# A hybrid decoder layer: an untaken branch moved from behind the expert loop to between its 26th and 27th block, and two of the closing row sums moved to TensorE

## The chip, the cores and the metric

The kernel runs on one NeuronCore of a Trainium2 chip. The metric is device time in microseconds (us) of one execution; the median of three runs stands for the kernel. About 0.5% (4 us) is what a measurement of this kernel can tell from no change.

## What is computed

One layer of a decoder trunk on 512 prompt rows and 8 sample rows of 1024 columns: a mixed attention and convolution stage, then a mixture of 32 experts of which each row uses 2, then a final RMSNorm. The change touches the end of the expert stage and the final norm only:

```python
hid = jax.nn.silu(jnp.einsum('nd,edf->nef', hf, w_gate)) * jnp.einsum('nd,edf->nef', hf, w_up)
y = jnp.einsum('nef,ne,efd->nd', hid, combine.astype(hid.dtype), w_down)
...
x = x + mods[5] * hier_moe(h, ...)
...
y_prompt = rmsnorm(xp, final_g)
y_sample = rmsnorm(xs, final_g)
```

## The kernel before, in words

The routed rows are sorted by expert into blocks of 64 rows. `run` (L1688) works off a list `todo` of 36 blocks: 6 experts whose weights were loaded ahead (blocks 0 to 5), then 4 experts with two blocks each (6 to 13), then 22 experts with one block each (14 to 35). An expert's weights are three tiles of 1 MB (`eg`, `eu`, `ed`), loaded by the SP queue (`weights`, L1609) into a rotating pool of 21 pages; a load waits until TensorE has used the page's former tile.

Two blocks share one gathered tile of 128 rows (`xg`, tiles `mA` and `mB` in the trace, two buffers). `gather` (L1626) is an indirect DMA that Pool issues. On TensorE, which works strictly in the order that `chain` and `in_turn` write down, a block is: `turned` (L1631, the gathered tile transposed in two halves, once for two blocks), `up` (L1643, 16 pairs of matmuls into `pgu`), `flip` (L1658) of the block before and `down` (L1667) of the block before. ScalarE applies Silu (`hidden`, L1655), VectorE multiplies; VectorE scales the result into `ot` (L1676) and Pool scatters it to `yrow` in DRAM with an indirect DMA (L1677).

Experts with more rows than their blocks hold would have left-over blocks. They sit in a branch (`tc.If(nxv > 0)`, L1731) behind the loop; in this data their number `nxi` is 0 and the branch isn't taken, but every engine loads the number, compares and jumps. Instructions of different engines are ordered by semaphores; where a branch isn't taken, each engine raises its semaphores by what the skipped code would have added. For Pool's DMA semaphores that is an instruction of its own, which the trace calls INC_SWDGE_SEM.

Then comes the closing stage (L1737 to L1795). SP loads the rows of `yrow` (two expert shares for each row, `yt`) when the scatters have landed; `xt` and the norm's gain `gf` were loaded before. For each of four tiles of 128 rows, `total` (L1752) adds `xt` and the two shares on VectorE and squares on ScalarE, Pool takes the inverse root (`pow`, L1765), and `final` (L1768) multiplies on VectorE and SP stores. `sample` (L1780) does the three additions and products for the 8 sample rows on Pool, between the tiles. `ORD` (L31) sets the order.

Of the kernel before, what the change touches and what calls it, by code (L numbers as in the profile page):

```python
# [9 lines left out]
F32 = mybir.dt.float32  # L10
# [3 lines left out]
AF = mybir.ActivationFunctionType  # L14
ALU = mybir.AluOpType
# [5 lines left out]
EPS = 1e-6  # L21
# [7 lines left out]
KTE = "VSSSSVVSSSSSSSVSSSSVVSSS"  # L29
GF_ = ()  # L30
ORD, ISS = "t0 t1 f0 t2 f1 s t3 q f2 f3", "fsq"  # L31
GT, TH, TF = (), (1, 1, 1, 2), (1, 1, 1, 2)
PLAN = ",c0,spread gn im sel,,,c1,k0 n cp,,,mc,,sn n3 n1 n0 n2,k1 rw,,,nq,,,,,,,,,,,,,cs,"
LU = (13, 15, 17)
EARLY = "CPXCACAXACAXCXAAICACAQCBIKI"
# [145 lines left out]
def body(tc, I, O, dbg=lambda *a: None):  # L181
# [1502 lines left out]
    def in_turn():  # L1684
        return tc.issue_after(chain[0].ins) if chain[0] is not None else ExitStack()


    def run(blocks, asks):  # L1688
        before = None
        for n, (b, W) in enumerate(blocks):  # L1690
            W = W()
            if n == 0:
                turned(b // 2, 0)
                turned(b // 2, 1)
            up(b, W, range(0, UP))
# [12 lines left out]
        down(*before)  # L1708

    pgus, hds, hTs_, scat = {}, {}, {}, []  # L1710
    chain = [lastw]
    asked = {0, OV0 // 2, NBLK // 2}
    gather(0)
# [2 lines left out]
    for j in range(NE):  # L1716
        hold = {}
        for _ in range(2 if NF <= j < NF + HV else 1):
            todo.append((len(todo), lambda j=j, hold=hold: hold.setdefault(0, hold.get(0) or weights(j))))
    run(todo, asked)  # L1720
    gfq = cp.tile([128, 256], F32, name="gfq", tag="c1")
    with tc.issue_after(mark["S"].ins):
        S.dma_start(gfq, I["GFQ"])
    gfb = page("gf")[:, 0:1024]
    SP.dma_start(gfb, I["GF"])
    xt = [page("xt0"), page("xt1")]
    for i in range(4):
        SP.dma_start(half(xt[i // 2], i % 2), xrow[128 * i:128 * i + 128])
    spare = [[page(f"sg{j}"), page(f"su{j}"), page(f"sd{j}")] for j in range(3)]
    nxv = nc.values_load(nxi[0:1, 0:1])  # L1730
    with tc.If(nxv > 0):  # L1731
        chain[0] = None
        gather(OV0 // 2)
        run([(b, lambda b=b: left(b - OV0)) for b in range(OV0, NBLK)], asked)


    ry = yrow.rearrange("(t a) f -> t (a f)", a=4)  # L1737
    ssf = cp.tile([128, 8], F32, name="ssf")
    rsf = cp.tile([128, 8], F32, name="rsf")
# [12 lines left out]
    def total(i):  # L1752
        t, t1, x = half(yt[i], 0), half(yt[i], 1), half(xt[i // 2], i % 2)
        (G if i in GT else V).tensor_tensor(x, x, t, op=ALU.add)
        n = 1024 // TH[i]
        for h in range(TH[i]):
            c = slice(n * h, n * h + n)
            op = V.tensor_tensor(t[:, c], x[:, c], t1[:, c], op=ALU.add)  # L1758
            S.activation(t1[:, c], t[:, c], AF.Square, scale=1.0 / 32, accum_out=ssf[:, 2 * i + h:2 * i + h + 1])  # L1759
        r = rsf[:, i:i + 1]  # L1760
        if TH[i] == 2:
            V.scalar_tensor_tensor(r, ssf[:, 2 * i:2 * i + 1], EPS, ssf[:, 2 * i + 1:2 * i + 2], op0=ALU.add, op1=ALU.add)
        else:
            V.tensor_scalar(r, ssf[:, 2 * i:2 * i + 1], EPS, None, op0=ALU.add)
        G.tensor_tensor(r, r, mh[:, 0:1], op=ALU.pow)  # L1765
        return op

    def final(i):  # L1768
        n = 1024 // TF[i]
        for h in range(TF[i]):  # L1770
            c = slice(n * h, n * h + n)
            t = half(yt[i], 0)[:, c]
            if i in GF_:
                S.activation(t, t, AF.Copy, scale=rsf[:, i:i + 1])
                G.tensor_tensor(t, t, gfb[:, c], op=ALU.mult)
            else:
                V.scalar_tensor_tensor(t, t, rsf[:, i:i + 1], gfb[:, c], op0=ALU.mult, op1=ALU.mult)  # L1777
            SP.dma_start(O[0][0, 128 * i:128 * i + 128, c], t)
# [6 lines left out]
    op = None
    for nm in ORD.split():
        with tc.issue_after(op.ins) if op is not None and nm[0] in ISS else ExitStack():
            r = (sample() if nm == "s" else quarter_rstd(rsf[:, 4:5], fs, 1.0 / D, EPS) if nm == "q" else
                 total(int(nm[1])) if nm[0] == "t" else final(int(nm[1])))
        if nm[0] == "t":  # L1790
            op = r
    V.scalar_tensor_tensor(fs, fs, rsf[:, 4:5], gfq, op0=ALU.mult, op1=ALU.mult)
# [26 lines left out]
```

## Time and profile before

| what | value |
|---|---|
| three runs | 795.72 us (median), 792.86, 796.38 |
| the profiled execution | 789.56 us, of it 787.8 us span |
| granted TensorE clock, mean | 0.944 of full speed |
| busy share of the span | TensorE 87%, VectorE 56%, ScalarE 27%, Pool 26% |
| HBM traffic | 267 GB/s over the span |

Times in the trace count from the span's start. "Releaser" is the work whose end let a waiting instruction go; a row's bracket gives the idle time of its engine before it. An instruction of a queue (SPq, POOLq, PEldq) is work of the engine's sequencer, not of the engine. Blocks of the expert loop are best counted by the ScalarE instruction `hd<-pgu` (L1655), which begins when a block's `up` is done: there are 36, from 522.1 to 746.7 us.

### The profile page before, as it was taken

Reading aid. Unit: us, or ns where it says so; the run is one execution under the profiler, and the core shown is the slowest. Engines: PE = TensorE matmul, PEld = TensorE weight load, DVE = VectorE, ACT = ScalarE, POOL = GpSimd, SP = SyncE. Lnnn points to the kernel's source line nnn. Section 1 sums busy time; section 2 is a strip of 40 time slices with the busy share of each in tenths; the row PEclk is TensorE's granted clock in tenths of the full one; section 3 lists DMA queues with packets and bytes.
Section 4 is the critical chain, followed back from the end, with each engine's and each line's share of the span. In section 5 each row is a group of like instructions: output and inputs, shape, how many; then the busy total and the mean of one; then the engine's idle time right before and its main releaser. Section 6 shows DMA issues by size and latency. Waiting matters only on the chain. (4 is left out here: it accounts for less than half of the span.)

```text
span 787.8 us, 12614 instructions
## 1 busy us (share of the span) xinstructions
PE 683.7 (87%) x4888; PEld 414.4 (53%) x4888; DVE 440.4 (56%) x960; ACT 213.7 (27%) x491; POOL 208.3 (26%) x182
## 2 busy tenths in 40 slices
PE   4999888997999988999789998289999999999910
PEld 3655777775786446644435444155555555554400
DVE  2444729999985758723776745843333333333245
ACT  1255721121113457634245323010110101010001
POOL 5134305035030101135602303312222222221114
PEclk9999999998999999999979999589999999999965
DMA  9985425644799303700004666679999999999954
GB/s 340 420 324 203 160 81 215 244 161 192 266 343 407 136 2 131 285 0 1 1 16 165 248 251 240 257 248 418 420 406 350 410 418 418 417 419 420 370 177 176
DMA packets 42332, 200.02 MB, mean 254 GB/s; under 512 B 10733, under 2 KB 14205, under 8 KB 22677
## 3 DMA queue, kind: packets, MB, share of 16 engines
q1 hardware_dynamic: 29341, 156.27, 50.7%
q0 software_dynamic: 10336, 40.95, 13.5%
q10 hardware_dynamic: 2592, 1.95, 0.8%
q8 instruction: 40, 0.66, 0.3%
q14 instruction: 23, 0.19, 0.1%
HBM read 187.82 MB, written 22.15 MB: 267 GB/s over the span
## 5 line engine op out<-in xcount | busy, mean ns | idle before, releaser
L591 DVE SCALAR_TENSOR_TENSOR y<-u,c,y 128x511 f32<-128x511 f32 (+23 forms) x120 | 103.7, 896 | 2.1
L1655 ACT ACTIVATE hd<-pgu 64x256 f32<-64x256 f32 x36 | 13.5, 375 | 200.4 <-PE pgu L1650 200.4
L1677 POOL DMA_INDIRECT yrow<-ot,six x36 | 39.1, 1085 | 99.4 <-DVE ot L1676 87.9
L1650 PE MATMUL pgu<-eu,mB 128*64 128x256 f32 x256 | 61.7, 384 | 1.9 <-DMA eu<-in_WU 1.9
L1650 PE MATMUL pgu<-eg,mB 128*64 128x256 f32 x256 | 62.2, 384 | 0.0
L1672 PE MATMUL pd<-ed,hTe 128*64 128x512 f32 x240 | 57.3, 598 | 0.8 <-issue 0.8
L1650 PE MATMUL pgu<-eu,mA 128*64 128x256 f32 x224 | 54.0, 384 | 1.8 <-DMA eu<-in_WU 1.8
L1650 PE MATMUL pgu<-eg,mA 128*64 128x256 f32 x224 | 54.2, 384 | 0.0
L1676 DVE SCALAR_TENSOR_TENSOR ot<-pd,wtb,mt 128x512 f32<-128x512 f32 x36 | 27.0, 751 | 44.3 <-PE pd L1672 44.3
L1656 DVE TENSOR_TENSOR hd<-pgu,hd 64x256 f32<-64x256 f32 x36 | 15.4, 428 | 59.1 <-ACT hd L1655 59.1
L1650 PEld LDWEIGHTS pgu<-eg,mB 128*64 128x64 f32 x256 | 32.8, 136 | 19.9 <-issue 5.1
L1381 ACT ACTIVATE P<-pSp,ast 128x128 f32<-128x128 f32 (+3 forms) x64 | 33.2, 534 | 24.2 <-DVE ast L1376 23.9
L1376 DVE TENSOR_REDUCE ast<-pSp 128x1 f32<-128x384 f32 (+3 forms) x44 | 27.3, 632 | 21.7 <-PE pSp L1371 21.6
L1650 PEld LDWEIGHTS pgu<-eg,mA 128*64 128x64 f32 x224 | 28.9, 136 | 17.3 <-issue 4.6
L225 DVE COPY hTe<-hTp 128x128 f32<-128x128 f32 x36 | 10.5, 291 | 48.3 <-PE hTp L1663 48.3
L370 PE MATMUL pr<-cTs,wc 128*64 128x256 f32 x256 | 37.1, 400 | 0.0
L1253 PE MATMUL woA<-wo,qT 128*128 128x512 f32 x64 | 35.9, 681 | 0.2 <-DVE rt L1175 0.2
L1650 PEld LDWEIGHTS pgu<-eu,mB 128*64 128x64 f32 x256 | 33.0, 136 | 4.0 <-DMA eu<-in_WU 2.8
L361 PE MATMUL cT<-CI,cR 128*128 128x128 f32 x128 | 21.1, 302 | 10.9 <-DVE cR L386 10.7
L1650 PEld LDWEIGHTS pgu<-eu,mA 128*64 128x64 f32 x224 | 28.9, 136 | 2.9 <-DMA eu<-in_WU 2.3
L1109 PE MATMUL woC<-wo,y 128*128 128x512 f32 x64 | 30.2, 605 | 0.1
L1413 PE MATMUL oT<-P,kv 128*64 128x512 f32 x80 | 28.6, 614 | 0.0
(572 smaller groups left out, 1654.5 us busy)
## 6 DMA issues: line engine op xcount, KB each, us to landing
eg<-in_WG SPq DMA_DIRECT2D x26, 1024.0 KB
eu<-in_WU SPq DMA_DIRECT2D x26, 1024.0 KB
ed<-in_WD SPq DMA_DIRECT2D x26, 1024.0 KB
wada<-in_WA SPq DMA_DIRECT2D x16, 1024.0 KB
wada<-in_WA POOLq DMA_DIRECT2D x8, 1024.0 KB, 15.2
WG<-in_WG SPq DMA_DIRECT2D x6, 1024.0 KB
WU<-in_WU SPq DMA_DIRECT2D x6, 1024.0 KB
WD<-in_WD SPq DMA_DIRECT2D x6, 1024.0 KB
```

What stands on the lines that cost most here:

```text
L361: PE.transpose(p[:, j, :], R[b:b + n, c, k, 2 * s8:2 * s8 + 2, :], ident[b:b + n, b:b + n])
L370: mark["PE"] = PE.matmul(self.pr[r][64 * c:64 * c + 64], wc1[:, c, 8 * r + 4 * h + s, :], self.T[h][:, c, s], start=(h == 0 and s == 0), s ...
L591: V.scalar_tensor_tensor(yb[:, s_:CVS], ub[:, :CVS - s_], w(k), yb[:, s_:CVS], op0=ALU.mult, op1=ALU.add)
L1109: PE.matmul(p, zc[:, g, 128 * i:128 * i + 128], wo[2 * n + 1][:, g], start=(g == 0), stop=(g == 3))
L1253: PE.matmul(pA, oTp[:, g, 128 * i:128 * i + 128], wo[2 * n][:, g], start=(g == 0), stop=(g == 3))
L1376: V.tensor_reduce(st[k][:, 0, h0:h0 + nh], pS[k][:, :nh * L].rearrange("p (h l) -> p h l", h=nh), axis=AX.X, op=ALU.max, negate=True)
L1381: S.activation(P[k][:, g, :L], pS[k][:, o:o + L], AF.Exp, bias=st[k][:, 0, g:g + 1], accum_out=st[k][:, 1, g:g + 1])
L1413: PE.matmul(oT[64 * k:64 * k + 64, :].rearrange("p (g t) -> p g t", g=4), kv12[:, br - 1, kt, 128 + 64 * k:192 + 64 * k], P[k][:, :, 128 * ...
L1650: chain[0] = PE.matmul(pgus[b][64 * h:64 * h + 64, :], xT[:, c, 64 * s_:64 * s_ + 64], w[:, c, :], start=(c == 0), stop=(c == 7))
L1672: chain[0] = PE.matmul(pd[64 * h:64 * h + 64, :], hT_[:, c, :], wd[:, c, 512 * h:512 * h + 512], start=(c == 0), stop=(c == 1))
L1676: V.scalar_tensor_tensor(ot, pd, wtb[:, b:b + 1], mt, op0=ALU.mult, op1=ALU.mult)
L1677: st = G.indirect_dma_start(out=yrow[:, :], out_offset=bass.IndirectOffsetOnAxis(ap=six[:, b:b + 1], axis=0), in_=ot, in_offset=None, boun ...
```

## The change

The list of blocks is cut after its first 26. `run` works off blocks 0 to 25, then the branch stands, then a second `run` works off blocks 26 to 35. The branch needs weight pages of its own; there were nine behind the loop, there are four now (`sg`, `su`, `sd0`, `sd1`), and they come out of the same rotating pool. Each `run` ends with its last block's `flip` and `down` and begins with its first pair's `turned`. In the closing stage, `yt` is loaded whole (four DMAs of 1 MB in place of eight of 512 KB), the sample rows are loaded by ScalarE's queue, and their work is on VectorE. The sums of tiles 0 and 2 (`TP`) are made by TensorE, as three matmuls with the unit matrix into one PSUM tile, for each half of the columns; VectorE adds tiles 1 and 3. The inverse roots of tiles 2 and 3 are taken by ScalarE's Sqrt and four small VectorE instructions; those of tiles 0 and 1 and of the sample rows stay on Pool. Orders on VectorE and ScalarE are written out (`dv`, `ac`).

```diff
-GT, TH, TF = (), (1, 1, 1, 2), (1, 1, 1, 2)
+LEFT, TP = 26, (0, 2)
...
-        S.activation(hd[64:128], pgu[0:64], AF.Silu)
+        silu[0] = S.activation(hd[64:128], pgu[0:64], AF.Silu)
...
-    run(todo, asked)
+    run(todo[:LEFT], asked)
+
+    sg, su = page("sg"), page("su")
+    spare = [[sg, su, page(f"sd{j}")] for j in range(2)]
+    nxv = nc.values_load(nxi[0:1, 0:1])
+    with tc.If(nxv > 0):
+        chain[0] = None
+        gather(OV0 // 2)
+        run([(b, lambda b=b: left(b - OV0)) for b in range(OV0, NBLK)], asked)
+        gather(LEFT // 2)
+    chain[0] = None
+    run(todo[LEFT:], asked)
...
-    spare = [[page(f"sg{j}"), page(f"su{j}"), page(f"sd{j}")] for j in range(3)]
-    nxv = nc.values_load(nxi[0:1, 0:1])
-    with tc.If(nxv > 0):
-        chain[0] = None
-        gather(OV0 // 2)
-        run([(b, lambda b=b: left(b - OV0)) for b in range(OV0, NBLK)], asked)
...
+    for q in range(4):
+        S.dma_start(ysq[32 * q:32 * q + 8].rearrange("p a (c j) -> p (a c) j", c=8),
+                    ry[512:520].rearrange("b (x r j) -> b x r j", r=4, j=32)[:, :, q])
     yt = [page(f"yt{i}") for i in range(4)]
     for i in range(4):
-        for j in range(2):
-            SP.dma_start(half(yt[i], j), ry[128 * i:128 * i + 128, 1024 * j:1024 * j + 1024])
-        if i == 1:
...
+        SP.dma_start(yt[i], ry[128 * i:128 * i + 128])
...
+        ac(t[:, 0:1], s_, AF.Sqrt)
+        dv(V.reciprocal, t[:, 1:2], t[:, 0:1])
+        dv(V.scalar_tensor_tensor, t[:, 0:1], s_, t[:, 1:2], t[:, 1:2], op0=ALU.mult, op1=ALU.mult)
+        dv(V.tensor_scalar, t[:, 0:1], t[:, 0:1], -0.5, 1.5, op0=ALU.mult, op1=ALU.add)
+        dv(V.tensor_tensor, r, t[:, 0:1], t[:, 1:2], op=ALU.mult)
...
+            if i in TP:
+                with in_turn():
+                    PE.matmul(py[i][h], ident, t0[:, c], start=False, stop=False)
+                    chain[0] = PE.matmul(py[i][h], ident, t1[:, c], start=False, stop=True)
+                z = py[i][h]
+            else:
+                dv(V.tensor_tensor, x[:, c], x[:, c], t0[:, c], op=ALU.add)
+                dv(V.tensor_tensor, x[:, c], x[:, c], t1[:, c], op=ALU.add)
+                z = x[:, c]
+            ac(jy[:, c], z, AF.Square, scale=1.0 / 32, accum_out=ssf[:, 2 * i + h:2 * i + h + 1])
...
+    sample()
+    total(0)
+    total(1)
+    sample_root()
+    root(0)
+    root(1)
+    total(2)
+    final(0)
+    dv(V.scalar_tensor_tensor, fs, fs, rsf[:, 4:5], gfq, op0=ALU.mult, op1=ALU.mult)
...
+        SP.dma_start(oq[:, :, q], fs[32 * q:32 * q + 8].rearrange("p (c j) -> p c j", c=8))
+    total(3, (0,))
+    final(1)
+    root(2)
+    total(3, (1,))
+    final(2)
+    root(3)
+    final(3)
```

How the order moves is seen at two places. On Pool, before, the last gathers and scatters (`yrow<-ot`) run through to the branch, and a gather is always issued one pair ahead of its use:

```order
L1627 DMA mA<-hrow,gix 128x1024
L1677 DMA yrow<-ot,six 2080x512 x2
L1627 DMA mB<-hrow,gix 128x1024
L1677 DMA yrow<-ot,six 2080x512 x8
L1730 TENSOR_LOAD nxi
L1731 COMPARE_AND_BRANCH
```

Now, behind the skipped code, Pool stands like this; ISA is the instruction that raises the semaphores, and DMASW are the semaphores of Pool's own DMAs:

```order
L1725 UNCONDITIONAL_BRANCH
L1725 ISA [waits DMASW4_49,DMASW5_49,DMASW3_49,DMASW6_49,DMASW2_49,DMASW7_49,DMASW1_49,DMASW0_49]
L1725 UNCONDITIONAL_BRANCH
L1627 DMA mA<-hrow,gix 128x1024 [waits DMASW5_49,DMASW4_49,PE_49]
L1627 DMA mB<-hrow,gix 128x1024 [waits DMASW6_49,PE_49]
L1627 DMA mA<-hrow,gix 128x1024 [waits DMASW7_49,DMASW5_49,PE_49]
L1677 DMA yrow<-ot,six 2080x512 [waits DMASW0_49,DVE_49]
```

The first gather of that piece fills `mA` for blocks 28 and 29. It stood well ahead of the 26th block's scatter before, and stands behind the wait for that scatter and behind ISA now.

On TensorE the place is the end of block 27 (the 28th), where the tile of blocks 28 and 29 is transposed; it comes ahead of block 26's `down`:

```order
L1650 MATMUL pgu<-eg_6751,mB 64x256
L1650 MATMUL pgu<-eu_6752,mB 64x256
L1640 MATMUL xTp<-CI,mA 128x128 [waits DMASW5_49,PE_49]
L1640 MATMUL xTp<-CI,mA 128x128 x3
L1672 MATMUL pd<-ed_6709,hTe 64x512 [waits DMAHW5_49,DVE_49]
L1672 MATMUL pd<-ed_6709,hTe 64x512 x3
L1640 MATMUL xTp<-CI,mA 128x128 [waits PE_49]
```

Within the second `run` the order of these rows is that of before; what moved is the gather that the first transpose waits for, and, ahead of block 26, the `flip` and `down` of block 25 and the branch.

## Rows read from the trace of the kernel before

**Rows 1.** Timeline of ScalarE, 677 to 747 us: start, duration, engine, line, operation, idle before

```profile
677.73 0.38 ACT L1655 ACTIVATE hd<-pgu 64x256 f32<-64x256 f32 x1 [5.21 <-PE pgu L1650]
...
684.79 0.38 ACT L1655 ACTIVATE hd<-pgu 64x256 f32<-64x256 f32 x1 [5.85 <-PE pgu L1650]
690.38 0.38 ACT L1655 ACTIVATE hd<-pgu 64x256 f32<-64x256 f32 x1 [5.21 <-PE pgu L1650]
...
697.44 0.38 ACT L1655 ACTIVATE hd<-pgu 64x256 f32<-64x256 f32 x1 [5.86 <-PE pgu L1650]
...
722.76 0.38 ACT L1655 ACTIVATE hd<-pgu 64x256 f32<-64x256 f32 x1 [5.88 <-PE pgu L1650]
730.82 0.38 ACT L1655 ACTIVATE hd<-pgu 64x256 f32<-64x256 f32 x1 [7.69 <-PE pgu L1650]
...
738.60 0.38 ACT L1655 ACTIVATE hd<-pgu 64x256 f32<-64x256 f32 x1 [6.54 <-PE pgu L1650]
746.73 0.38 ACT L1655 ACTIVATE hd<-pgu 64x256 f32<-64x256 f32 x1 [7.76 <-PE pgu L1650]
```

**Rows 2.** Windows, 650 to 700 us: busy time of engines, then granted clock, DMA share, GB/s

```profile
650.00:700.00 50.00, 50.00 (x367) 26.04 (x363) 17.69 (x36) 5.39 (x12) 12.69 (x12) 1.00 1.02 417
```

**Rows 3.** Waits of the SP queue, 652 to 727 us: total, times, longest

```profile
SPq L1616 <- DMA eg<-in_WG: 23.5, 9, 5.4
```

**Rows 4.** Instructions of the branch's line: times, ns min/median/max, first and last start

```profile
L1731 POOLq EVENT_SEMAPHORE  x4: 17/42/43, 755.5 to 755.7; - x4
...
L1731 PEldq COMPARE_BRANCH  x1: 3987/3987/3987, 750.1 to 750.1; - x1
...
L1731 POOLq INC_SWDGE_SEM  x1: 1996/1996/1996, 755.8 to 755.8; - x1
```

**Rows 5.** Timeline of TensorE around blocks 27 and 28

```profile
690.23 0.66 PE L1640 MATMUL xTp<-CI,mA 128*128 128x128 f32 x4
690.82 1.94 PE L1672 MATMUL pd<-ed,hTe 128*64 128x512 f32 x8
```

**Rows 6.** Timeline of Pool: the gather for blocks 28 and 29, the last scatter

```profile
668.33 1.11 POOL L1627 DMA_INDIRECT mA<-hrow,gix  x1 [4.94 <-PE xTp L1640]
...
752.48 0.98 POOL L1677 DMA_INDIRECT yrow<-ot,six  x1 [1.79 <-DVE ot L1676]
```

**Rows 7.** Tile `yrow`, 480 to 790 us: start of a scatter to its landing

```profile
DMA to landing us min/median/max: 2.6/7.2/10.1
```

**Rows 8.** Tile `mA`, 480 to 790 us: start of a gather to its landing

```profile
DMA to landing us min/median/max: 3.4/8.7/10.0
```

**Rows 9.** Windows around an idle stretch of TensorE, columns as in rows 2

```profile
187.50:193.25 5.75, 0.00 (x0) 0.00 (x1) 5.61 (x7) 2.00 (x2) 3.61 (x2) 0.83 0.32 112
193.25:198.10 4.85, 4.85 (x22) 4.85 (x23) 4.85 (x7) 0.00 (x0) 1.84 (x1) 0.50 0.00 0
```

**Rows 10.** Timeline of the SP queue in the closing stage

```profile
757.77 1.75 SPq L1745 DMA_DIRECT2D yt<-yrow  x4
```

**Rows 11.** Timeline of VectorE in the closing stage

```profile
763.40 1.22 DVE L1758 TENSOR_TENSOR yt<-xt,yt 128x1024 f32<-128x1024 f32 x1 [0.24 <-DMA yt<-yrow]
...
771.97 1.74 DVE L1777 SCALAR_TENSOR_TENSOR yt<-yt,rsf,gf 128x1024 f32<-128x1024 f32 x1
...
775.98 1.29 DVE L1758 TENSOR_TENSOR yt<-xt,yt 128x512 f32<-128x512 f32 x2
...
778.45 0.15 DVE L1762 SCALAR_TENSOR_TENSOR rsf<-ssf 128x1 f32<-128x1 f32 x1
...
779.50 1.42 DVE L1777 SCALAR_TENSOR_TENSOR yt<-yt,rsf,gf 128x512 f32<-128x512 f32 x2
```

**Rows 12.** Timeline of TensorE at full clock: one f32 matmul of 128 by 512, two passes

```profile
446.53 1.12 PE L1253 MATMUL woA<-wo,qT 128*128 128x512 f32 x2
```

**Rows 13.** Timeline of ScalarE in the closing stage

```profile
777.34 0.61 ACT L1759 ACTIVATE yt<-yt 128x512 f32<-128x512 f32 x1
```

**Rows 14.** Line L1795, the sample rows' stores: ns min/median/max, first and last start

```profile
L1795 ACTq DMA_DIRECT2D out<-fs x4: 692/701/1226, 779.5 to 782.2; - x4
```

More of the change, by code (lines that the diff above doesn't have):

```diff
@@ L1708, in run @@
         down(*before)
-    pgus, hds, hTs_, scat = {}, {}, {}, []
+    pgus, hds, hTs_, scat, silu = {}, {}, {}, [], [None]
     chain = [lastw]
@@ L1719, in body @@
             todo.append((len(todo), lambda j=j, hold=hold: hold.setdefault(0, hold.get(0) or weights(j))))
-    run(todo, asked)
+    run(todo[:LEFT], asked)
[9 more added lines that the diff above has]
+    run(todo[LEFT:], asked)
     gfq = cp.tile([128, 256], F32, name="gfq", tag="c1")
-    with tc.issue_after(mark["S"].ins):
+    with tc.issue_after(silu[0].ins):
         S.dma_start(gfq, I["GFQ"])
@@ L1739, in body @@
     rsf = cp.tile([128, 8], F32, name="rsf")
-    ysq = mid("ysq").rearrange("p (a f) -> p a f", a=2)
-    V.memset(ysq, 0.0)
+    rtt = cp.tile([128, 8, 2], F32, name="rtt")
+    ysq = page("ysq")[:, 0:512].rearrange("p (a f) -> p a f", a=2)
+    jy = page("jy")
+    with tc.issue_after(mark["V"].ins):
+        V.memset(ysq, 0.0)
+    with tc.issue_after(silu[0].ins):
+        S.activation(rsf[:, 5:6], one, AF.Sqrt)
+    for q in range(4):
+        S.dma_start(ysq[32 * q:32 * q + 8].rearrange("p a (c j) -> p (a c) j", c=8),
+                    ry[512:520].rearrange("b (x r j) -> b x r j", r=4, j=32)[:, :, q])
@@ L1742, in body @@
     yt = [page(f"yt{i}") for i in range(4)]
     for i in range(4):
-        for j in range(2):
-            SP.dma_start(half(yt[i], j), ry[128 * i:128 * i + 128, 1024 * j:1024 * j + 1024])
-        if i == 1:
-            for q in range(4):
-                SP.dma_start(ysq[32 * q:32 * q + 8].rearrange("p a (c j) -> p (a c) j", c=8),
-                             ry[512:520].rearrange("b (x r j) -> b x r j", r=4, j=32)[:, :, q])
-    fs = small("fs")
[L1752 to L1766, printed above, removed]
@@ L1768, in final @@
-    def final(i):
[L1769 to L1778, printed above, removed]
-    def sample():
-        G.tensor_tensor(fs, ysq[:, 0], ysq[:, 1], op=ALU.add)
-        G.tensor_tensor(fs, fs, m5s, op=ALU.mult)
-        G.tensor_tensor(fs, fs, x1s, op=ALU.add)
@@ L1785, in body @@
[L1785 to L1792, printed above, removed]
+        SP.dma_start(yt[i], ry[128 * i:128 * i + 128])
@@ new lines, in body, with ac, dv, inv_root @@
+    fs = small("fs")
+    row, arow = [None], [None]
+    def ac(*a, **k):
+        with tc.issue_after(arow[0].ins) if arow[0] is not None else ExitStack():
+            arow[0] = S.activation(*a, **k)
+    def dv(f, *a, **k):
+        with tc.issue_after(row[0].ins) if row[0] is not None else ExitStack():
+            row[0] = f(*a, **k)
+    def inv_root(i):
+        s_, r, t = ssf[:, 2 * i:2 * i + 1], rsf[:, i:i + 1], rtt[:, i]
+        if i < 2:
+            G.tensor_tensor(r, s_, mh[:, 0:1], op=ALU.pow)
+            return
+        ac(t[:, 0:1], s_, AF.Sqrt)
[3 more added lines that the diff above has]
+        dv(V.tensor_tensor, r, t[:, 0:1], t[:, 1:2], op=ALU.mult)
@@ new lines, in body, with total @@
+    cols = [slice(512 * h, 512 * h + 512) for h in range(2)]
+    py = {}
+    with in_turn():
+        for i in TP:
+            py[i] = [acc("py") for _ in range(2)]
+            for h, c in enumerate(cols):
+                chain[0] = PE.matmul(py[i][h], ident, half(xt[i // 2], i % 2)[:, c], start=True, stop=False)
+    def total(i, hs=(0, 1)):
+        t0, t1, x = half(yt[i], 0), half(yt[i], 1), half(xt[i // 2], i % 2)
+        for h in hs:
+            c = cols[h]
+            if i in TP:
+                with in_turn():
+                    PE.matmul(py[i][h], ident, t0[:, c], start=False, stop=False)
[6 more added lines that the diff above has]
+            ac(jy[:, c], z, AF.Square, scale=1.0 / 32, accum_out=ssf[:, 2 * i + h:2 * i + h + 1])
@@ new lines, in root @@
+    def root(i):
+        s_ = ssf[:, 2 * i:2 * i + 1]
+        dv(V.scalar_tensor_tensor, s_, s_, EPS, ssf[:, 2 * i + 1:2 * i + 2], op0=ALU.add, op1=ALU.add)
+        inv_root(i)
+    def final(i):
+        for h, c in enumerate(cols):
+            z = py[i][h] if i in TP else half(xt[i // 2], i % 2)[:, c]
+            o = half(yt[i], 0)[:, c]
+            dv(V.scalar_tensor_tensor, o, z, rsf[:, i:i + 1], gfb[:, c], op0=ALU.mult, op1=ALU.mult)
+            if i > 1:
+                SP.dma_start(O[0][0, 128 * i:128 * i + 128, c], o)
+        if i < 2:
+            SP.dma_start(O[0][0, 128 * i:128 * i + 128], half(yt[i], 0))
@@ new lines, in body, with sample_root @@
+    ssq = e2.tile([128, 2], F32, name="st", tag="st")
+    def sample():
+        dv(V.tensor_tensor, fs, ysq[:, 0], ysq[:, 1], op=ALU.add)
+        dv(V.tensor_tensor, fs, fs, m5s, op=ALU.mult)
+        dv(V.tensor_tensor, fs, fs, x1s, op=ALU.add)
+        ac(small("jks"), fs, AF.Square, accum_out=ssq[:, 0:1])
+    def sample_root():
+        p = tps("qs", (128, 1))
+        PE.matmul(p, sel, ssq[:, 0:1], start=True, stop=True)
+        dv(V.tensor_scalar, ssq[:, 1:2], p, 1.0 / D, EPS, op0=ALU.mult, op1=ALU.add)
+        G.tensor_tensor(rsf[:, 4:5], ssq[:, 1:2], mh[:, 0:1], op=ALU.pow)
@@ L1793, in body @@
+    sample()
[7 more added lines that the diff above has]
+    dv(V.scalar_tensor_tensor, fs, fs, rsf[:, 4:5], gfq, op0=ALU.mult, op1=ALU.mult)
     oq = O[1].rearrange("b t (c r j) -> (b t) c r j", r=4, j=32)
     for q in range(4):
-        S.dma_start(oq[:, :, q], fs[32 * q:32 * q + 8].rearrange("p (c j) -> p c j", c=8))
+        SP.dma_start(oq[:, :, q], fs[32 * q:32 * q + 8].rearrange("p (c j) -> p c j", c=8))
+    total(3, (0,))
+    final(1)
```

## The prediction

> **What bounds the kernel now.** I read the slices of the page first, in which TensorE and the DMA engines are both nearly full over the expert loop. Then ScalarE's timeline, where each `hd<-pgu` marks the end of a block's `up` [rows 1]. Blocks come in pairs: 7.06 us (684.79 after 677.73), then 5.59 us (690.38 after 684.79). The last three blocks are longer: 730.82 is 8.06 after 722.76 in place of 5.60, 738.60 is 7.78 later in place of 7.06, 746.73 is 8.13 later in place of 5.60. TensorE loses 2.46 + 0.72 + 2.53 = 5.7 us there, waiting for weights. The weights come at 417 GB/s with the DMA engines full from 650 to 700 us [rows 2], and SP waits for landings of earlier loads, not for pages (23.5 us in 9 waits on `eg` alone) [rows 3]. So the loop starts bound by TensorE and ends bound by the weight stream. A delay of TensorE in the middle is free up to 5.7 us, and costs its full length beyond.
>
> The third view is the branch's own line [rows 4]. Behind the loop TensorE leaves its compare at 750.1 + 3.99 = 754.1, which is 7.4 us after the last `hd`. Pool waits for the last scatter until 755.5, begins INC_SWDGE_SEM at 755.8 and needs 2.0 us for it. SP's first `yt` load goes out at 757.77 [rows 10], when that ends at 757.8, though the scatter, started at 752.48 [rows 6], landed 2.6 us later, at 755.1 [rows 7].
>
> **The branch in the middle: TensorE.** The part up to block 25 is unchanged; its `hd` is at 677.73 [rows 1]. Then comes what stood behind block 35: rest of the `down` before, `flip`, `down`, load, compare. By the 7.4 us above TensorE is through at 685.1. The weight stream is fuller here than at 750, so this may be later; it doesn't matter as long as it stays under the wait below. Two half transposes of 0.66 [rows 5] and the copy behind them take about 1.5 us; block 26 without any `down` takes 5.6 - 1.9 - 0.3 = 3.4 (1.94 is a `down` [rows 5], 0.3 the `flip`, an estimate: two transposes where the 0.66 has four). Its `hd` comes at 690.0, and block 27's `up`, with a `flip`, ends 3.7 later, at 693.7. There TensorE wants the tile of blocks 28 and 29.
>
> **The branch in the middle: Pool, the main term.** That tile was gathered at 668.33 before [rows 6], 22 us ahead of its transposes at 690.23 [rows 5]. Now its gather is the first Pool instruction behind the branch. The last scatter starts 752.48 - 746.73 = 5.75 us behind its block's `hd` [rows 1, 6]; for block 25 that is 683.5. It lands 7.2 us later by the median [rows 7]: 690.7. (2.6, the least, is of the idle DMA engines at the end; 10.1 the most.) From landing to INC_SWDGE_SEM 755.8 - 755.1 = 0.7, for INC itself 2.0 [rows 4]: Pool issues the gather at 693.4. By the median of 8.7 [rows 8] it lands at 702.1 (bounds: 3.4 on idle engines, 10.0). So TensorE stands from 693.7 to 702.1. From the transposes to the next `hd` it is 697.44 - 690.23 = 7.2 us [rows 1, 5], so block 28's `hd` comes at 709.3 in place of 697.44: 11.9 us late. The next gather follows the first at once, since its buffer is free from 686.7, and waits for nothing more.
>
> **The clock.** After a stretch of 5.75 us without a matmul TensorE worked the next 4.85 us at a granted 0.50, the 1.2 GHz level [rows 9]; half of that time is lost, 2.4 us. The stall of 8.4 us is longer, so I add 2.4 (bounds 0, if the clock holds, and twice that). Late in all: 14.3 us. The weight stream gives back 5.7: **+8.6 us** at the end of the loop. Bounds: with 5.1 less for scatter and gather together (the scatter landing after 5.1 and the gather after 5.7, both between the least and the median) and no clock loss, 11.9 - 5.1 - 5.7 = +1.1; with 10.1 and 10.0 for the medians and twice the clock loss, 11.9 + 4.2 + 4.8 - 5.7 = +15.2.
>
> **The pages.** Four pages of the rotating pool lie idle around the branch, so the weights of ten blocks are asked for 4 MB later than before, about 10 us of the stream at 417 GB/s [rows 2]. At each of those issues SP waited for the landing of an earlier load [rows 3]; its loads go round on eight semaphores (DMAHW0 to 7), so eight were outstanding, 8 MB or 20 us of the stream. Asked for 10 us later they still stand in a queue, so I cost this at nothing. If that cover were gone, the stream would lose what the queue is short of, up to the 10 us.
>
> **The closing stage.** Three terms.
> - Start: no INC in front of `yt`. SP goes at 755.1 in place of 757.77, relative to the last scatter: -2.6 (bounds -2.0, if the semaphore is seen as late as Pool saw it, and -2.7).
> - The work, counted from the first `yt` issue. Before: 779.50 + 1.42 - 757.77 = 23.2 us [rows 10, 11]. After: the first whole `yt` tile is there after 763.40 - 757.77 = 5.6. TensorE then needs four matmuls. A matmul of this size takes 1.12 at full clock [rows 12], and less, some 0.95, in a row; TensorE has stood idle for about 6 us again, so I take two at half speed: 5.7, to 11.3. One more square of 0.61 and tile 1's two [rows 13] bring 13.2, and then VectorE is free to finish: final sums of tile 3 in four halves, 2.6 (1.29 for two [rows 11]); four finals of 1.42 [rows 11], 5.7; the sample rows' product, 0.5, an estimate from the 0.65 of half a tile; two roots. A root through Pool takes 1.05 now (778.45 to 779.50 [rows 11]); the new one is a Sqrt and five small VectorE instructions of 0.15 each that follow one another over two engines: 1.7, an estimate (bounds 1.0 and 2.4). Sum 13.2 + 2.6 + 5.7 + 0.5 + 3.4 = 25.4: +2.2 (bounds +0.3 with TensorE at full clock, +4).
> - End: the stores of `fs` were issued by ScalarE until 782.2 + 0.7 [rows 14], behind the last `final` at 780.92; now they leave earlier, from SP. -1.0 (bounds 0 and -1.6).
> Together -1.4, between -4.0 and +2.0. What VectorE sheds, tiles 0 and 2's adds, and what Pool's three sample steps cost it (1.74 for a product that takes 1.42 in two halves [rows 11]) is in this sum already: the stage is now held by roots in series, not by adds.
>
> **Sum.** +8.6 - 1.4 = +7.2 us on the profiled execution's 789.56, or 796.8. The runs' median of before is 6.2 us above that execution; on it the forecast is 795.72 + 7.2 = **802.9 us**, and all times below are on it.
>
> **A rule that speaks against the change.** Row: TensorE's compare and jump took 3.99 us [rows 4], far over the time of any other instruction there, so leaving skipped code has a price here. The sum has it for TensorE, where it hides under the gather's wait; it has none for Pool, whose jump back stands between INC and the gather. The Trainium skill, "Runtime: NRT & Kernel Launch", section "Instruction fetch mechanics", says that a taken branch to a page that isn't loaded must fetch it by DMA before execution goes on. By that rule Pool pays for a fetch too, and the result is the first rival below; no row shows Pool's jump by itself.
>
> **The rivals.**
> 1. *Pool also waits for code.* Between INC and the gather, Pool's jump costs up to what TensorE's did, 4.0 us [rows 4]. For: that row. Against: Pool's code behind the branch is short. Time 802.9 + 4.0 = 806.9.
> 2. *The gather comes soon enough.* Scatter and gather land nearer to their least values, TensorE's stall is short and the clock holds: +1.1 - 1.4, time 795.4. For: Pool has two scatters only 3 us apart and nothing else queued. Against: medians of 7.2 and 8.7 under a full weight stream [rows 7, 8].
> 3. *The weights still end the loop, faster.* TensorE is no more than 5.7 us late at block 28, that is, its tile is there by 695.9: the loop ends when it did, and only the closing stage counts. At that stage's better bound, 795.72 - 4.0 = 791.7. For: three terms of the stage point down. Against: INC alone ends at 693.4, and a gather in 2.5 us is under the least seen, 3.4 [rows 8].
> 4. *The page loss bites.* It would show as the stream falling under 417 GB/s [rows 2] behind block 26 and add to the forecast; it lies in the upper range.
>
> **How the numbers follow.** Forecast 0.58, rival 1 with 4 0.12, rival 2 0.22, rival 3 0.08. The forecast's own range is 799 to 808. Over all, 794.0 to 808.5 leaves out most of rival 3 and a tenth of the forecast and the upper rivals. Slower by over 0.5% (above 799.7): nearly all of forecast and rivals 1 and 4, 0.67. Within 0.5%: rival 2 and the forecast's low edge, 0.25. Faster by over 0.5% (under 791.7): 0.08.
>
> **What would show it.** Right: a wait of some 8 us of TensorE at the first transpose of `mA` behind the branch, its releaser the gather; a lower granted clock in the few us behind it; INC_SWDGE_SEM of 2 us on Pool near 691; the last blocks no longer waiting for `eu`; `yt` issued within 3 us of the last scatter's start. Wrong: no such wait of TensorE, or the last blocks still waiting for weights; then the loop ends as before. If VectorE's last `final` ends less than 23 us after the `yt` issue, the closing stage was mis-sized.

## The result and the profile after

The changed kernel takes **801.16 us** (median of 20 runs); the kernel before, beside it, 793.76 us (20 runs). The ratio is 1.0086, 95% interval 1.0067 to 1.0106: slower by 0.9%, some 6.8 us (the two medians lie 7.4 apart). The forecast was 802.9 us on a median of 795.72, a ratio of 1.0090.

The profiled executions differ by more: spans 801.0 and 787.8 us. But `hd` of block 25, up to which TensorE's work is unchanged, starts at 682.57 after the change and at 677.73 before [rows 1]. These 4.8 us lie ahead of the change: over all fourteen kernels below, each profiled once, that start lies anywhere from 675.5 to 683.4. Everything below is counted from that `hd`. Four terms then cover the rest, each between rows of the timeline: **loop** (`hd` of block 25 to that of block 35), **start** (to SP's first `yt` issue), **work** (to the end of the last `final`), **end** (to the end of the span). Each figure is rounded by itself.

| us | loop | start | work | end | sum |
|---|---|---|---|---|---|
| before | 69.0 | 11.0 | 23.1 | 6.9 | 110.0 |
| after | 76.1 | 8.7 | 30.1 | 3.5 | 118.4 |
| difference | +7.1 | -2.4 | +7.0 | -3.4 | +8.3 |
| forecast | +8.6 | -2.6 | +2.2 | -1.0 | +7.2 |

**The loop.** ScalarE's timeline of the changed kernel, to be held against [rows 1]:

```profile
682.57 0.38 ACT L1655 ACTIVATE hd<-pgu 64x256 f32<-64x256 f32 x1 [5.21 <-PE pgu L1650]
...
704.22 0.38 ACT L1655 ACTIVATE hd<-pgu 64x256 f32<-64x256 f32 x1 [4.71 <-PE pgu L1650]
708.09 0.38 ACT L1655 ACTIVATE hd<-pgu 64x256 f32<-64x256 f32 x1 [3.49 <-PE pgu L1650]
...
715.15 0.38 ACT L1655 ACTIVATE hd<-pgu 64x256 f32<-64x256 f32 x1 [5.92 <-PE pgu L1650]
...
753.07 0.38 ACT L1655 ACTIVATE hd<-pgu 64x256 f32<-64x256 f32 x1 [5.83 <-PE pgu L1650]
758.66 0.38 ACT L1655 ACTIVATE hd<-pgu 64x256 f32<-64x256 f32 x1 [5.21 <-PE pgu L1650]
```

Block 26 follows block 25 by 21.65 us instead of 7.06. Block 28 comes 32.58 us after block 25 instead of 19.71, 12.9 late; from there the pairs keep 7.06 and 5.6 to the last, so the waits for weights at the end, 5.7 us before, are gone. What made block 26 late stands in TensorE's waits, 677 to 765 us (releaser, total, times, longest), in those of SP's queue, 652 to 735 us, in the instructions of the branch's line (now L1725), in Pool's timeline and in three windows:

```profile
PE xTp L1640 <- DMA yrow<-ot,six: 10.5, 1, 10.5
```

```profile
SPq L1616 <- PE pgu L1650: 30.7, 8, 8.7
SPq L1616 <- DMA yrow<-ot,six: 9.5, 1, 9.5
```

```profile
L1725 POOLq EVENT_SEMAPHORE  x4: 17/43/1732, 693.9 to 695.8; - x4
...
L1725 PEldq COMPARE_BRANCH  x1: 6156/6156/6156, 685.9 to 685.9; - x1
...
L1725 POOLq INC_SWDGE_SEM  x1: 1716/1716/1716, 695.9 to 695.9; - x1
```

```profile
688.31 0.98 POOL L1677 DMA_INDIRECT yrow<-ot,six  x1 [1.80 <-DVEq L1725]
698.56 1.04 POOL L1627 DMA_INDIRECT mA<-hrow,gix  x1 [9.26 <-DMA yrow<-ot,six]
```

```profile
687.30:697.70 10.40, 0.00 (x0) 0.00 (x1) 1.28 (x2) 0.00 (x0) 0.98 (x1) 0.69 1.02 416
697.70:701.40 3.70, 3.67 (x18) 2.61 (x20) 0.69 (x1) 0.60 (x1) 2.05 (x2) 0.50 1.01 418
701.40:706.00 4.60, 4.60 (x46) 2.94 (x42) 0.43 (x1) 0.38 (x1) 0.00 (x0) 1.00 1.01 411
```

Pool's steps are those of the forecast: the scatter of block 25 starts 5.74 us behind its `hd`, Pool waits for its landing, raises its DMA semaphores (INC_SWDGE_SEM, 1.7 us, to 697.6), and issues the gather into `mA` 15.99 us behind the `hd` (forecast 15.7). TensorE's wait is somewhere else: not at `mA` but at the first transposes of `mB` (697.73), directly behind the branch, and it ends with INC. The profile names a scatter, `yrow`, as releaser, which those transposes do not read: what they share with it is one of Pool's DMA semaphores. (That the branch's writing of `mB` ties them to INC is shown by e3 and e4 below.) TensorE then works 3.70 us at granted 0.50, the 1.2 GHz level, and loses 1.85 us by it.

SP's queue stood for INC as well: a load of `eg` waited 9.5 us and went out at 697.72, the load ahead of it at 687.28. Its other waits are now mostly for pages that TensorE still uses (30.7 us in 8 waits on `pgu`), where before they were for landings [rows 3]. The weight stream does not notice either: 411 to 418 GB/s here, 417 from 697 to 740.

**The closing stage.** VectorE's timeline of the changed kernel, and the DMA queues in two stretches of it (packets, MB, share):

```profile
763.40 0.75 DVE L1676 SCALAR_TENSOR_TENSOR ot<-pd,wtb,mt 128x512 f32<-128x512 f32 x1 [1.08 <-PE pd L1672]
781.34 0.43 DVE L1768 TENSOR_TENSOR fs<-ysq 128x256 f32<-128x256 f32 x1 [17.19 <-DMA ysq<-yrow]
...
782.61 2.74 DVE L1768 TENSOR_TENSOR xt<-xt,yt 128x512 f32<-128x512 f32 x4
...
796.05 1.41 DVE L1768 SCALAR_TENSOR_TENSOR yt<-xt,rsf,gf 128x512 f32<-128x512 f32 x2
```

From 772 to 779 us, while `yt` is loaded on SP's queue (q1) and `ysq` on ScalarE's (q10):

```profile
q1 hardware_dynamic: 374, 2.79, 99.0%
q10 hardware_dynamic: 159, 0.02, 2.0%
```

From 779 to 781.3 us, with all but the last 0.12 MB of `yt` landed:

```profile
q1 hardware_dynamic: 30, 0.12, 13.3%
q10 hardware_dynamic: 249, 0.03, 8.7%
```

The sample rows' 64 KB are 512 packets of 128 bytes (q10 also moves a few others). Beside the 4 MB of `yt` they pass at 159 in 7 us, behind it at 249 in 2.3 us, so they are whole only when all of `yt` is. VectorE's first closing instruction is the one that reads them, and stands from 764 to 781.34, though tile 1 had very likely landed nearly 6 us sooner (e5 below shows it 8.2 us after the first `yt` issue, which would be 775.5 here). Behind it, in order: ScalarE's squares, TensorE's small matmul and so the sums of tile 2.

**The end.** The last line's instructions (L1815 before, L1873 after), Pool's DRAIN and SP's:

```profile
L1815 POOLq DRAIN  x3: 51/109/8255, 778.6 to 787.5; - x3
L1815 SPq DRAIN  x3: 7/7/13, 784.5 to 787.2; - x3
```

```profile
L1873 POOLq DRAIN  x3: 51/109/8170, 786.4 to 800.7; - x3
L1873 SPq DRAIN  x3: 7/7/13, 800.0 to 800.4; - x3
```

DRAIN is an instruction that every engine has at the program's end. Pool's first one takes 8.2 us in both kernels, and starts about when Pool's last operation does. Before, that was tile 3's root, and the DRAIN ran from 778.6 to 786.9, 2.4 us past SP's own first one; the span ended 0.9 later. Now Pool's last operation is tile 1's root, the DRAIN runs from 786.4 to 794.6, and SP's wait for the last stores, to 800.0, sets the end. So the end is shorter because Pool works earlier; no step of the forecast had it. What takes the DRAIN its 8 us, no run shows.

### The profile page after: what moved, and what is told of

It is laid out like the page before. It is cut to its first block, busy times and chain, and to the rows that moved or that the text cites. A ratio compares the mean times of both kernels' runs of the same rounds, so it can differ in the third digit from the quotient of the medians.

```text
span 801.0 us, 12677 instructions
## 1 busy us (share of the span) xinstructions
PE 703.8 (88%) x4912; PEld 424.9 (53%) x4912; DVE 438.3 (55%) x973; ACT 216.0 (27%) x501; POOL 202.8 (25%) x177
## 4 chain that ended last, share of the span: by engine, by line
PE 46%; DVE 22%; issue 15%; DMA 8%; POOL 4%; ACT 3%; ACTq 0%; POOLq 0%; DVEq 0%
DVE y L591 11%; PE pgu L1650 6%; PE pr L370 5%; DMA yrow<-ot,six 4%; PE woC L1109 3%; PE oT L1413 3%; PE woA L1253 3%; PE pS L956 3%; POOL yrow L1677 3%; PE cT L361 3%; PE pd L1672 2%; PE pTp L1403 2%; PE pkv L727 2%; PE pT L966 2%; DMA ysq<-yrow 1%
## 5 line engine op out<-in xcount | busy, mean ns | idle before, releaser
L591 DVE SCALAR_TENSOR_TENSOR y<-u,c,y 128x511 f32<-128x511 f32 (+23 forms) x120 | 101.9, 882 | 2.1
L225 DVE COPY hTe<-hTp 128x128 f32<-128x128 f32 x36 | 10.5, 291 | 42.4 <-PE hTp L1663 41.0
```

Of the source, the lines that this page charges most:

```text
L591: V.scalar_tensor_tensor(yb[:, s_:CVS], ub[:, :CVS - s_], w(k), yb[:, s_:CVS], op0=ALU.mult, op1=ALU.add)
```

## The experiments

All ratios are to the kernel before, run beside. The terms are those of the table above, from each one's profiled execution. Where terms and ratio differ, the ratio is the measurement; sums of single executions stray from it by up to some 4 us.

| run | loop | start | work | end | sum | ratio, 95% interval |
|---|---|---|---|---|---|---|
| e1_branch_only | 75.9 | 8.1 | 23.6 | 6.9 | 114.5 | 1.0072, 1.0042 to 1.0102 |
| e2_closing_only | 69.0 | 11.2 | 30.9 | 3.5 | 114.5 | 1.0038, 1.0010 to 1.0065 |
| e3_mA_only | 76.6 | 9.1 | 30.4 | 3.5 | 119.6 | 1.0099, 1.0065 to 1.0134 |
| e4_own_tile | 71.5 | 9.0 | 30.3 | 3.5 | 114.3 | 1.0040, 1.0010 to 1.0070 |
| e9_short_body | 69.4 | 8.1 | 30.4 | 3.5 | 111.3 | 1.0002, 0.9968 to 1.0036 |
| e5_sample_late | 76.0 | 8.5 | 26.6 | 3.5 | 114.6 | 1.0053, 1.0024 to 1.0083 |
| e6_ysq_on_sp | 75.8 | 9.0 | 25.6 | 3.5 | 113.9 | 1.0007, 0.9975 to 1.0038 |
| e10_no_tensor_sums | 75.9 | 8.1 | 29.9 | 3.5 | 117.4 | 1.0113, 1.0066 to 1.0160 |
| e7_own_tile_late | 71.7 | 8.8 | 26.9 | 3.5 | 110.9 | 0.9992, 0.9961 to 1.0023 |
| e8_closing_late | 69.2 | 11.8 | 26.8 | 3.5 | 111.3 | 0.9969, 0.9938 to 0.9999 |
| e11_own_tile_best | 71.6 | 8.6 | 25.4 | 6.9 | 112.4 | 1.0021, 0.9988 to 1.0054 |
| e12_behind_best | 69.6 | 11.2 | 25.6 | 6.9 | 113.2 | 1.0017, 0.9982 to 1.0051 |

**Which half loses? e1 and e2.** The change was cut in two. e1 is the kernel before with `run(todo, asked)` replaced by the change's lines from `run(todo[:LEFT], asked)` to `run(todo[LEFT:], asked)`, and its own branch behind the loop taken out. e2 is the changed kernel with the branch put back behind the loop (a Sqrt that loads ScalarE's table ahead of time also moves behind the sample rows' loads):

```diff
-    run(todo[:LEFT], asked)
...
-        gather(LEFT // 2)
-    chain[0] = None
-    run(todo[LEFT:], asked)
+    run(todo, asked)
...
+    with tc.If(nxv > 0):
+        chain[0] = None
+        gather(OV0 // 2)
+        run([(b, lambda b=b: left(b - OV0)) for b in range(OV0, NBLK)], asked)
```

> The kernel before with the moved branch alone; its closing stage is the old one, all on VectorE, ScalarE and GpSimd. Theory (the branch costs what the trace after shows at it): TensorE waits about 10.5 us at the first transpose of mB behind the branch, hd of block 35 comes 76 us after hd of block 25 instead of 69.0 (+7.1), the first yt load is issued 2.4 us sooner after hd of block 35 (8.7 instead of 11.0), and the closing work is as before: +4.7 us against the kernel before, ratio 1.006. Rival (the loss of the change is the closing stage's, and a later end of the loop is given back there): within 0.2% of the kernel before. A wait at mA as I forecast would show as an idle time at the transposes of mA instead.

> The new closing stage alone, with the branch behind the loop as before. Theory (the closing stage costs what the trace after shows): the sample rows' small loads, issued by ScalarE beside the yt loads, land only with the last of yt, VectorE's first closing instruction waits for them, the work from the first yt issue to the last final takes about 30 us instead of 23.2 (+7.0), the stores end 3.3 us sooner, the start stays at 11.0 us: +3.7 us against the kernel before, ratio 1.0047. Rival (my forecast's terms: work +2.2, end -1.0): +1.2 us, ratio 1.0015.

Both lose, each by about what was expected: 1.0072 and 1.0038. TensorE's wait in e1 is that of the changed kernel, at `mB`:

```profile
PE xTp L1641 <- DMA yrow<-ot,six: 10.1, 1, 10.1
```

The loop term of e1 and the work term of e2 are within 0.8 us of those of the changed kernel. Work is nearly unchanged in e1 (23.6 against 23.1), loop and start in e2.

**Why TensorE waits at `mB`: e3 and e4.** Pair 13 is gathered into `mB` ahead of the branch, but the branch's own pairs go into `mA` and `mB` too, and pair 13 is gathered again at its end. In e3 the branch writes only `mA`, in e4 neither:

```diff
+    bx, lx = page("bx"), list(xg)
...
         chain[0] = None
+        xg[:] = [half(bx, 0), half(bx, 1)]
         gather(OV0 // 2)
...
-        gather(LEFT // 2)
+        xg[:] = lx
```

(e4; in e3 the added line in the branch is `xg[1] = half(bx, 0)`. With the tiles free, the gather of pair 14 stands ahead of the branch on Pool in e4.)

> The change, but the pairs that the branch would gather into mB go into a page of their own, and pair 13 is not gathered again; mA is still written in the branch. Theory (the wait at mB comes only from mB being written in the branch): TensorE idles less than 1 us at the first transposes of mB behind the branch apart from the jump; then the gather of pair 14, issued 16 us after hd of block 25, comes too late and the wait that I forecast appears at the first transposes of mA, some 8 us; hd of block 28 comes 34 us after hd of block 25 (after: 32.6), so +1.4 us against the change, ratio to the kernel before 1.010. Rival (TensorE waits for the raise of Pool's semaphores whatever is written in the branch): the 10.5 us stay at mB and the time is that of the change, 1.0086.

> The change, but all pairs of the branch are gathered into a page of their own, pair 13 is not gathered again, and the gather of pair 14 stands ahead of the branch on Pool. Theory: neither mB nor mA waits for Pool any more; TensorE loses only its drain and jump at the branch (some 4 to 6 us), which the weights' lead gives back; hd of block 35 comes 69 to 71 us after hd of block 25 (after: 76.1): 5 to 7 us below the change, ratio to the kernel before 1.000 to 1.003. Rival (scatters that pile up behind Pool's wait, or TensorE's own jump, cost the same): no more than 1 us below the change, ratio 1.007 or above.

TensorE's timeline, first transposes of each tile behind the branch, in e3 and then in e4:

```profile
685.20 1.94 PE L1640 MATMUL xTp<-CI,mB 128*128 128x128 f32 x8 [5.04 <-PEq L1726]
...
699.77 0.63 PE L1640 MATMUL xTp<-CI,mA 128*128 128x128 f32 x4 [3.31 <-DMA mA<-hrow,gix]
```

```profile
690.40 1.94 PE L1640 MATMUL xTp<-CI,mB 128*128 128x128 f32 x8 [4.98 <-PEq L1726]
```

The wait at `mB` hangs on what the branch writes: it is gone in both. In e3 the wait that I had forecast comes out, at `mA`, for its gather, 3.3 us instead of some 8 because TensorE gets there later; block 28 comes 33.1 us after block 25 (expected 34), and the time is the change's or a little more. In e4 both are gone and the loop ends 4.6 us sooner. That is a little less than the 5 to 7 us expected, and the ratio, 1.0040, is above the expected 1.000 to 1.003 (its interval reaches down to 1.0010). What remains at the branch is 5.0 us of TensorE standing at its own jump.

**What the jump costs: e9.** The body cut from 16 left-over blocks to one:

```diff
-        run([(b, lambda b=b: left(b - OV0)) for b in range(OV0, NBLK)], asked)
+        run([(b, lambda b=b: left(b - OV0)) for b in range(OV0, OV0 + 1)], asked)
```

> The kernel with the branch's own page, and the body of the branch cut from all left-over blocks to one (the others are left out; the branch is not taken with this input). What is left of TensorE's loss there is its compare-and-branch of 6.0 us. If the jump's price hangs on the length of the code that is jumped over, it falls to 2 us or less and the loop ends some 2 us sooner (hd of block 35 at 69 to 70 us after that of block 25, ratio 1.001). If the price is that of fetching the code at the target, whatever lies between, it stays at 5.5 to 6.5 us and the time is that of the own page, ratio 1.004.

The branch's line in e4, then in e9:

```profile
L1726 PEldq COMPARE_BRANCH  x1: 5976/5976/5976, 684.1 to 684.1; - x1
L1726 DVEq COMPARE_BRANCH  x1: 72/72/72, 686.2 to 686.2; - x1
```

```profile
L1726 PEldq COMPARE_BRANCH  x1: 236/236/236, 686.3 to 686.3; - x1
...
L1726 DVEq COMPARE_BRANCH  x1: 72/72/72, 688.3 to 688.3; - x1
```

TensorE's compare and jump falls from 5.98 to 0.24 us, its idle time there from 5.0 to 0.3, and the loop ends where it ended before. My wording of the second case, that the price is the target's whatever lies between, is refuted: what is jumped over decides. That the fetch of code is what takes the time is in line with the queues: in the 8 us around the jump of e4 two packets move on the instruction queues, in e9 none. The Trainium skill, "Runtime: NRT & Kernel Launch", section "Instruction fetch mechanics", says that a taken branch to code that is not already in the engine's window of pages must fetch it first; TensorE's rows agree, with 5.98 against 0.24 us. VectorE's 0.07 is the same in both; whether its target lay in its window, no run shows. One thing is not as clean as it looks: with the short body the scatter of block 25 went behind the branch on Pool, so the loop term of e9 is not the jump's alone.

**Why the closing work is long: e5 and e6.** e5 only moves lines; e6 puts the sample rows' loads on SP's queue, between the second and the third `yt` load:

```diff
-    sample()
     total(0)
     total(1)
-    sample_root()
     root(0)
     root(1)
     total(2)
     final(0)
+    final(1)
+    sample()
+    sample_root()
+    total(3, (0,))
...
-    total(3, (0,))
-    final(1)
```

```diff
-    for q in range(4):
-        S.dma_start(ysq[32 * q:32 * q + 8].rearrange("p a (c j) -> p (a c) j", c=8),
-                    ry[512:520].rearrange("b (x r j) -> b x r j", r=4, j=32)[:, :, q])
...
         SP.dma_start(yt[i], ry[128 * i:128 * i + 128])
+        if i == 1:
+            for q in range(4):
+                SP.dma_start(ysq[32 * q:32 * q + 8].rearrange("p a (c j) -> p (a c) j", c=8),
+                             ry[512:520].rearrange("b (x r j) -> b x r j", r=4, j=32)[:, :, q])
```

> The change with one move in the closing stage's order: the work on the sample rows (sample, sample_root and their product) stands behind the finals of tiles 0 and 1, so nothing waits for the sample rows' loads that could run before them. Theory (in the change everything stands in order behind VectorE's wait for the sample rows, which land with the last of yt): VectorE starts on tile 1 some 7 us after the first yt issue instead of 14 us, and what is left behind the sample rows' landing is 10.5 us of instructions instead of 16: some 5.5 us below the change, ratio to the kernel before 1.001 to 1.003. Rival (the closing work is long because of TensorE's slow sums and the root chains, whatever the order): within 1.5 us of the change, ratio 1.007 to 1.010.

> The change with the order kept, but the sample rows' four loads are issued by SyncE between the second and third yt load, as in the kernel before. Theory: they land some 8 us after the first yt issue as before, not 14, so VectorE's first closing instruction starts 5 to 6 us sooner; the two last yt loads are issued 3.6 us later and bound the last tile: 4 to 5 us below the change, ratio to the kernel before 1.002 to 1.004. Rival (small packets land late beside large loads whichever queue issues them): the sample rows still land behind the last yt load, no gain or a loss by the later yt loads, ratio 1.008 to 1.013.

VectorE's first closing rows, in e5 (first `yt` issue at 767.70) and in e6 (760.96):

```profile
775.91 2.75 DVE L1768 TENSOR_TENSOR xt<-xt,yt 128x512 f32<-128x512 f32 x4 [11.21 <-DMA yt<-yrow]
```

```profile
770.46 0.43 DVE L1769 TENSOR_TENSOR fs<-ysq 128x256 f32<-128x256 f32 x1 [13.01 <-DMA ysq<-yrow]
```

In e5 tile 1 is added 8.2 us after the first `yt` issue, not 15.3; work falls by 3.5 us, less than the 5.5 expected (ratio 1.0053, not 1.001 to 1.003); the sample rows' chain over three engines (783.53 to 786.0) now stands in the middle, which is a likely reason. In e6 the sample rows are there 9.5 us after the issue, not 14.0, beside the same large loads and with the same small packets, and work falls by 4.5. They were issued at nearly the same times, up to 3.8 us after the first `yt` load in e6 and up to 3.6 us in the changed kernel. So their place in the queues decides: behind two large loads in one queue they are through before the third (by 769 us all of them, with 2.3 of the 4.2 MB of `yt`), on a queue of their own they trickle until nearly all four are. A queue of their own with the last two `yt` loads held back was not tried. The ratio 1.0007 is better than the terms give; what the runs bear out is that most of the closing stage's loss, 4.5 of 7.0 us, was this one wait. The other 2.5 us were not taken apart; `yt` in four loads in place of eight, for one, was not tried alone.

**Do TensorE's sums pay? e10.** e6 with `LEFT, TP = 26, ()`, so that VectorE adds all four tiles.

> The change with the sample rows' loads on SyncE, and all four tiles' sums on VectorE (none on TensorE). Theory (VectorE is what bounds the closing work once the sample rows are there: 16 us of instructions in order behind tile 1's landing): two more totals of 2.7 us, one of them before tile 1 lands, so 3 to 5 us above the kernel with the loads on SyncE, ratio to the kernel before 1.004 to 1.007. Rival (TensorE's sums, which start at half clock, cost as much as they take off): within 1 us of it, ratio 0.999 to 1.003.

Work rises by 4.3 us (25.6 to 29.9), as expected; the ratio rises from 1.0007 to 1.0113, past the expected 1.004 to 1.007 and by more than the terms give, as e6's lies below them. By the terms, TensorE's sums pay nearly what VectorE would need for two totals, 2 x 2.7, although TensorE's first two of these matmuls take 2.07 and 1.91 us in the changed kernel, where later ones take 1.02.

**Repairs: e7, e8, e11, e12.** e7 is e4 with e5's order, e8 is e2 with it. e11 (from e4) and e12 (from e2) take more together: `TP = (1, 2)`, `ysq` on SP, the sample rows' operations and all roots on Pool, the sample rows finished late:

```diff
+    total(0)
+    total(1)
+    root(0)
+    final(0)
+    sample()
+    total(2)
+    root(1)
+    final(1)
+    sample_root()
+    total(3)
...
-        if i < 2:
+        if i < 4:
...
-        dv(V.tensor_tensor, fs, ysq[:, 0], ysq[:, 1], op=ALU.add)
+        G.tensor_tensor(fs, ysq[:, 0], ysq[:, 1], op=ALU.add)
```

> Both repairs: the branch gathers into a page of its own and the sample rows' work comes late. Theory, by adding the two: loop end 2.5 us later than in the kernel before (71.5 us from hd of block 25 to that of block 35, as measured with the own page), start of the closing stage 2.0 sooner, closing work and end 1.8 sooner: 1.3 us below the kernel before, ratio 0.998. If the two repairs do not add up (the time then being set by another wait), 1.002 or above.

> The branch behind the loop as before, the new closing stage with the sample rows' work late. Theory: the closing stage alone was measured 4.4 us longer than before from hd of block 35 to the end in its trace (45.6 against 41.0); the late sample rows take 5.5 off: 1 us below the kernel before, ratio 0.998 to 1.000. Rival (TensorE's sums and the root chains make it long): ratio 1.003 or above.

> A repaired version with the branch where the change has it: own page in the branch; sample rows' loads on SyncE; TensorE sums tiles 1 and 2 in place of 0 and 2, so VectorE can start on tile 0 as soon as it lands; the sample rows' three operations and all roots on GpSimd; the sample rows finished behind the finals of tiles 0 and 1. Theory: loop end 71.6 us after hd of block 25 (before 69.0), start of the closing 9.0 (11.0), work from the first yt issue to the last final 21 us (23.2; change 30.1), end 3.5 (6.9): 4.9 us below the kernel before, ratio 0.994. If VectorE beside GpSimd is slowed or TensorE's half clock sets the tiles' sums, work 23 to 24 us and ratio 0.997.

> The same closing stage with the branch behind the loop as before. Theory: loop 69.0 and start 11.2 as before, work 21, end 3.5: 5.4 us below the kernel before, ratio 0.993; the same as with the moved branch and the own page within the measurement. If the moved branch is worth its place once the wait is gone, this one comes out 2 us or more above that one.

e7 adds up: e4's loop and e5's work stand in one kernel, and the ratio is 0.9992, no loss left, no gain either. e8 comes out at 0.9969, its interval just under 1, and is the best of all; its terms do not show a gain over before, so I take it for "not slower". e11 and e12 missed by 6 to 7 us. They have the same closing stage and differ in the branch's place, and come out alike (1.0021 and 1.0017): with TensorE's wait for INC gone, moving the branch still gains nothing, as e7 and e8 say too. No version is clearly faster than the kernel before. Work in e11 is 25.4, not 21: VectorE stood 3.4 us for tile 1's squares, and those for its sums on TensorE, whose first three matmuls took 2.08, 1.91 and 1.91 us (1.02 later). VectorE's timeline of e11:

```profile
772.98 0.16 DVE L1771 SCALAR_TENSOR_TENSOR ssf<-ssf 128x1 f32<-128x1 f32 x1 [3.43 <-ACT jy L1767]
```

And the end is 6.9 again, as in e1 and before, because the last root is on Pool once more (781.25). The last line's instructions of e11:

```profile
L1876 POOLq DRAIN  x3: 51/109/8030, 781.2 to 789.8; - x3
L1876 SPq DRAIN  x3: 7/7/13, 786.7 to 789.5; - x3
```

That was not meant as a test of Pool's DRAIN, but it is one: of the fourteen kernels, the four whose last Pool operation starts 2 us before the last `final` is done (before, e1, e11, e12) end at 6.9, and the ten where it starts 8 us or more before that end at 3.5. The version that would follow, e6's loads in e4 with the last two roots left on ScalarE and VectorE, was not tried; by the terms it is at 71.6 + 9.0 + 25.6 + 3.5 = 109.7, level with before.

## Why the prediction was right, and where it was not

The sign and the size came out: +6.8 us measured by the ratio (+8.3 by the terms), +7.2 forecast, 801.2 us in the range. The main term, Pool's chain at the branch, was the right mechanism; part of the agreement is luck, as the steps show:

- **Pool's chain: right.** Scatter, landing, INC, gather: 15.99 us against 15.7.
- **TensorE in the middle: wrong place.** The step "Two half transposes of 0.66 and the copy behind them take about 1.5 us" let TensorE go on with pair 13's tile. It had to wait there for INC, since the branch writes that tile too (e1, e3, e4). The forecast had looked at the transposes of `mA` only. The price hardly changes: 12.9 us late at block 28 against 14.3 (e3, which has the forecast's wait: 13.3). Both waits hang on the same Pool chain, but that the rest is alike is chance: the forecast has the gather's 8.7 us between INC and the transposes of `mA`, the changed kernel has blocks 26 and 27, 10.4 us from 697.7 to 708.1.
- **TensorE's jump: hidden, as costed,** though it took 6.2 us in place of 4.0, under the longer wait for Pool; with that wait gone it is the next one (5.0 us, e4).
- **Clock: right,** 1.85 against 2.4 us. **Given back by the weights: right,** 5.8 against 5.7. **Pages: right,** the stream stays at 416 and 417 GB/s, even with SP's queue standing 9.5 us for INC, which the forecast did not have.
- **Start: right,** -2.4 against -2.6.
- **Work: mis-sized, +7.0 against +2.2.** The step that failed is the count from the first `yt` tile over TensorE and the squares: it had nothing for the sample rows, which the new order puts first on VectorE and whose loads land last on a queue of their own. With the loads back on SP, 4.5 us of the 7.0 are gone (e6), and the 25.6 left are near the forecast's 25.4, though not by the same steps. "The stage is now held by roots in series, not by adds" was wrong too: two more tiles added on VectorE cost 4.3 us (e10).
- **End: mis-sized, -3.4 against -1.0,** and for another reason: Pool's DRAIN, not the stores of `fs`.

The two errors in the closing stage, +4.8 and -2.4, and the loop's -1.5 partly cancel; the sum was better than its parts, and that is luck. The first rival, Pool waiting for code like TensorE, did not happen at its price: from INC's end at 697.6 to the gather is 0.95 us, not 4. The second and third needed a loop that ends at most 1.1 us later; it ended 7.1 later. The fourth had the stream fall; it did not.

## What to carry to other kernels

A branch that is never taken can still stop an engine or a queue that next uses a tile, a page or rows written inside it, until Pool has raised the semaphores for the skipped work: here TensorE for 10.5 us, SP's weight loads for 9.5, and the first `yt` load in the kernel before. Give skipped code tiles of its own (e4), and keep it short: TensorE's jump took 5.98 us over the long body and 0.24 over the short one (e9). Small loads that the first instruction of a stage needs belong into the queue of the large ones, at the place where they are wanted, not beside them. Look at what ends last in the span's final 10 us before pricing a stage's end: there it was an 8-us DRAIN of an engine that had nothing left to do.

## What the runs showed of the hardware that I had not expected

- TensorE's compare and jump: 3.99 us over the full body with nearly idle DMA engines [rows 4], 5.98 and 6.16 us in a full weight stream (e4, after), 0.24 over a body of one block (e9); VectorE, ScalarE and Pool 0.05 to 0.07.
- Pool's first DRAIN at the end: 8.0 to 8.4 us from about the start of its last operation, in all fourteen kernels.
- 128-byte packets on a second queue beside loads of whole 8-KB rows: 23 per us, against 108 per us once those had all but landed (after, queue q10).
